# A dependent sum in VectorE's order moved behind one other instruction

## The chip, the cores and the metric

The kernel runs on one core of one Trainium2 chip. A core has a matrix engine (TensorE, PE in the profile), a vector engine (VectorE, DVE), a scalar engine (ScalarE, ACT), GpSimd (POOL) and SyncE (SP), each with its own queue of instructions that it works off in order, and sixteen DMA engines that move data between HBM and the core's memory. The metric is the device time of one execution in microseconds (us), as a median over runs.

## What is computed

Two layers of a bidirectional encoder over 256 tokens of width 4096. What matters here is the shape of the large products, all in float32:

```python
for l in range(DEPTH):                       # DEPTH = 2
    h = rmsnorm(x, norm_w[l])
    proj = h @ w_in[l]                       # (256 x 4096) @ (4096 x 11264)
    aq, ak, av, ag, rq, rk, rv, rg = jnp.split(proj, SPLIT_POINTS, axis=-1)
    a_out = silu(ag) * gqa_attention(rope(norm(aq)), rope(norm(ak)), av)
    r_out = silu(rg) * rmsnorm(bidirectional_retention(rope(rq), rope(rk), rv))
    x = x + concat(a_out, r_out) @ w_out[l]  # (256 x 4096) @ (4096 x 4096)
return rmsnorm(x, final_norm)
```

The two weight matrices are nearly all of the input, and each of their elements is read once.

## The kernel before

**Products.** The depth of 4096 is cut into 16 pairs of 128-row slices (NP = 16), the output columns into blocks of two times 512, the tokens into two halves of 128. One pair of one block is a 2 x 2 by 2 x 2 product of blocks. For some pairs it is done with eight block products, for the others ("seven" pairs) with seven, after a Winograd scheme: there the weights' four blocks, in two pages "raw" and "other", are also combined into two more pages on VectorE, called wsum in the profile: v (tag T, one subtraction over 128x1024), and u (tag U, two instructions over 128x512). With a the raw page and b the other one, u's first half is a[1] + v[0], and its second half is u's first half minus b[1]. So v, the first half and the second half are a chain, each step reading what the step before it wrote.

**Precision.** A float32 operand is split into a rounded high part and the remainder. ScalarE casts the high part (whi, or whb for a half page), VectorE subtracts to get the low part (wlo, wlb), and TensorE does three products of 512 columns per block product: whi with the operand's high part, whi with its low part, wlo with the high part. So each weight page costs one cast on ScalarE and one subtraction on VectorE. For pages called "far", ScalarE makes fhi and the negative flo, and a DMA that adds, issued by GpSimd, completes flo.

**The token operands** (x7h, x7l, x8h, x8l, xmh, xml) are made once for each of the four phases (in and out projection of two layers) by `split_pair` (L929): for a seven pair VectorE makes four sums s1 to s4 into a page xf, ScalarE casts the high parts, and VectorE subtracts the low parts.

**What sets the order.** Python code plans the whole program once, before anything runs. `run` keeps one clock for each engine (class `Clock`, with costs of instructions), always takes the engine that is free first, and `pick` (L867) records the next instruction for it. Work on weights is held in lists of `Op`s by engine, sorted by due time; `Weights.best` (L754) looks at the first LOOK = 4 entries of VectorE's list and takes the first that is ready. Everything else (combining the seven products M1 to M7 at the end of a block, rotary tables, attention, retention, operand splits) runs as `Lane`s, that are put between the weight work by their due times or their urgency. The chip then runs each engine's list in that order, with semaphores where data or a buffer is waited for. A wait on one row of VectorE holds all rows behind it.

**Buffers.** There are six raw pages of 512 KB (RAWS), four whi (HIGHS), three wlo (LOWS), one pair of half pages (HALVES), two wsum pages (SUMS) and two far pages (FAR). A raw page's next load is issued by SyncE's queue when its last reader is done. The raw page of a seven group has two readers that count: u and wlo.

In `Weights.make_u`, that is the whole step before:

```python
ve.tensor_add(u[:, 0, :], a[:, 1, :], v[:, 0, :])
ve.tensor_sub(u[:, 1, :], u[:, 0, :], b[:, 1, :])
g.u = (u, Ready(now, ve.done))
```

Of the kernel before, what the change touches and what calls it, by code (L numbers as in the profile page):

```python
# [40 lines left out]
HALVES = 1  # L41
SUMS = 2
FAR = 2
LOOK = 4
DUE_LEAD = 25.0
RUSH, SPLIT_LEAD = 2.8, 6.0
SUMS_PACE = 7.0
# [3 lines left out]
SUM_LEAD = 2.0  # L51
# [176 lines left out]
class Clock:  # L228


    def __init__(self, engine, cost, lap, now):
        self._engine, self._cost, self._lap, self._now = engine, cost, lap, now
        self.until, self._wrote = 0.0, None

    @property
    def done(self):
# [2 lines left out]
    def __getattr__(self, name):  # L239
        call = getattr(self._engine, name)  # L240

        def recorded(out, *args, **kwargs):
            self.until = max(self.until, self._now.t)
            if self._wrote and any(meet(self._wrote, extent(v)) for v in sources(args, kwargs)):
                self.until += self._lap + OWN_PASS
            self.until += self._cost(name, out, args, kwargs) - self._lap
            self._wrote = extent(out)
            return call(out, *args, **kwargs)  # L248

        return recorded  # L250
# [70 lines left out]
def extent(v):  # L321
    return v.tensor.name, v.offset, v.offset + sum(step * (n - 1) for step, n in list(v.ap)[1:])
# [24 lines left out]
def hybrid_encoder(  # L347
# [17 lines left out]
    ve = Clock(nc.vector, vector_cost, 0.083, now)  # L365
# [29 lines left out]
    def f32(v):  # L395
        return v.bitcast(F32)
# [37 lines left out]
    one = t(cp, [P, P], "one")  # L434
# [98 lines left out]
    class Weights:  # L533


        def __init__(self):
            self.pages, at = [], 0.0
            for phase in range(2 * DEPTH):
                w = w_out if phase % 2 else w_in
                for b in range(N_OUT2 if phase % 2 else N_IN):  # L540
                    start = (phase, b) == (0, 0)
                    end = (phase, b) == (2 * DEPTH - 1, N_OUT2 - 1)
                    for n, (p, k, uses) in enumerate(pages_in_order(phase, start, end)):
                        g = Page()
# [12 lines left out]
            self.lows, self.halves = Slots(LOWS), Slots(HALVES)  # L557
            self.holds = {"x7": Slots(0), "x8": Slots(0)}
            self.todo, self.ops = [], {"V": [], "A": [], "F": []}
            at = {}  # L560
            for g in self.pages:
                if g.direct:
                    self.todo.append((g.at, g, "raw", g.kind == PAGE_B))
                    continue
                if not g.seven:
                    self.todo.append((g.at - (FAR_LEAD if g.far else 0.0), g, "raw", g.kind == PAGE_B))
                    if g.far:
                        self.op("F", g, FAR_LEAD, self.far_ready, self.far_parts)
                    else:
                        self.op("A", g, HIGH_LEAD, self.high_ready, self.high)  # L570
                        self.op("V", g, 0.0, self.low_ready, self.low)
                    continue
                if g.kind == PAGE_A:
                    a = g
                    a.raw = a.other = a.v = a.u = None
                    a.reads = {PAGE_A: 2, PAGE_B: 2}
                    self.todo.append((g.at, a, "raw", 0))
                    self.todo.append((g.at + 0.01, a, "other", 1))
                    self.op("V", a, SUM_LEAD, self.v_ready, self.make_v)
                    self.op("V", a, SUM_LEAD - 0.01, self.u_ready, self.make_u)  # L580
                g.a = a
                self.op("A", g, HIGH_LEAD, self.high_ready, self.high)
                self.op("V", g, 0.0, self.low_ready, self.low)
            self.todo.sort(key=lambda v: v[0])
            for v in self.ops.values():
                v.sort(key=lambda o: o.key)
            self.at, self.adds, self.landed = 0, [], {}

        def place(self):
            return self.pages[self.at].at if self.at < len(self.pages) else 1e9  # L590
# [29 lines left out]
        def make_v(self, g):  # L620
            self.sums.take()
            a, b = f32(g.raw[0]), f32(g.other[0])
            v = t(wp, [P, 2, NB], "wsum", SUMS)
            ve.tensor_sub(v, a, b[:, 0:1, :].to_broadcast([P, 2, NB]))
            g.v = (v, Ready(now, ve.done))

        def u_ready(self, g):
            return g.v is not None and self.sums.ready()

        def make_u(self, g):  # L630
            self.sums.take()
            a, b, v = f32(g.raw[0]), f32(g.other[0]), g.v[0]
            u = t(wp, [P, 2, NB], "wsum", SUMS)
            ve.tensor_add(u[:, 0, :], a[:, 1, :], v[:, 0, :])
            ve.tensor_sub(u[:, 1, :], u[:, 0, :], b[:, 1, :])
            g.u = (u, Ready(now, ve.done))
            for k in (PAGE_A, PAGE_B):
                g.reads[k] -= 1
                if not g.reads[k]:
                    self.raws.give(ve.done)  # L640
# [113 lines left out]
        def best(self, engine):  # L754

            if engine == "A":
                ops = [o for o in self.ops["A"][:1] + self.ops["F"][:1] if o.ready()]
            else:
                ops = [o for o in self.ops["V"][:LOOK] if o.ready()][:1]
            return min(ops, key=lambda o: o.key, default=None)  # L760

        def make(self, one):
            self.ops[one.engine].remove(one)
# [2 lines left out]
    weights = Weights()  # L766
# [99 lines left out]
    def pick(e):  # L866
        if e == "P":  # L867
            if step_lane("P", lanes + running()):
                return True
            if main[1] is not None and main[1]():  # L870
                progress[0] = now.t
                main[1] = next(main[0], None)
                return True
            return False
        if step_lane(e, urgent):
            return True
        w = weights.best(e)
        splits = [v for v in waiting[:SPLITS] if v.ready(e)]
        soon = splits[0] if splits else None
        hurry = [v for v in lanes + running() if v.ready(e) and v.urge()]  # L880
        first = min((v for v in lanes + running() if v.ready(e)), key=lambda v: v.due, default=None)
        if soon and (w is None or soon.key - SPLIT_LEAD < w.key):
            soon.step()
        elif first and w and first.due < w.key:
            first.step()
        elif hurry and (w is None or w.key > weights.place() + RUSH):
            hurry[0].step()
        elif w:
            weights.make(w)
        else:  # L890
            return step_lane(e, splits + lanes + running())
        clear()
        return True
# [40 lines left out]
    def split_pair(p, v, phase, gains):  # L934

        def tokens(v):

            return v.rearrange("p k (a t) -> p k a t", t=BLK)

        x0, x1 = v[:, 0], v[:, 1]  # L940
        if gains is not None:
            yield "A"
            for i in range(2):
                u = v[:, :, i].rearrange("p m a t -> p (a m) t" if phase else "p m a t -> p m (a t)")
# [4 lines left out]
        if seven:  # L949
            yield lambda: not sums_of and held[0] + sum(max(0, v.need - v.own) for v in tasks if v.begun) < PAGES  # L950
            sums_of.append(p)
            hi, lo = (t(ap, [P, blocks, P], tag + s, n, F32R) for s in "hl")
# [4 lines left out]
            ac.copy(tokens(hi[:, 0:2, :]), x0)  # L957
            yield "V"
            ve.tensor_sub(s1, a22n, x1[:, 0])
            ve.scalar_tensor_tensor(s2, s1, -1.0, x0[:, 0], op0=ALU.mult, op1=ALU.subtract)  # L960
            ve.tensor_sub(s3, x0[:, 0], x1[:, 0])
            ve.tensor_sub(s4, x0[:, 1], s2)
            yield "A"
            ac.copy(hi[:, 2:7, :], f)
            yield "V"
            ve.tensor_sub(tokens(lo[:, 0:2, :]), x0, tokens(f32(hi)[:, 0:2, :]))
            ve.tensor_sub(lo[:, 2:7, :], f, f32(hi)[:, 2:7, :])
            sums_of.pop()
            drop()
        else:  # L970
            hi, lo = (t(ap, [P, blocks, P], tag + s, n, F32R) for s in "hl")
            u = [w[:, :4].rearrange("p (i m) (a t) -> p i m a t", i=2, t=BLK) for w in (hi, lo)]
            g = [tokens(w[:, 4:6]) for w in (hi, lo)]
# [1078 lines left out]
```

## Time and profile before

| | |
|---|---|
| median of 3 runs | 2584.46 us (2583.87 to 2585.4) |
| the profiled execution | 2583.31 us, of which the span from the first to the last instruction is 2581.3 us |
| granted TensorE clock, mean | 0.998 of full |
| TensorE busy | 2565.5 us, 99% of the span |
| VectorE busy | 2318.1 us, 90% |
| ScalarE busy | 1912.0 us, 74% |
| GpSimd busy | 445.3 us, 17% |
| DMA | 727.53 MB, 282 GB/s; its packets took 91.8% of the time of sixteen engines |

A matmul row of the timeline gives start and duration. Matmuls overlap in TensorE's pipeline: one of 512 columns is shown 0.39 us long, and the next one starts 0.23 us after it. So time that TensorE loses is best read from the distance between two starts, and only a part of it is shown as an idle time in brackets. On VectorE the shown durations overlap as well: a row that doesn't read what the row before it wrote starts about 0.08 us before that one's shown end. In the names, "wsum<-wraw" over 1024 elements is v, "wsum<-wraw,wsum" u's first half, "wsum<-wsum,wraw" its second half. L248 is the line of `Clock.recorded`, through which all VectorE and ScalarE work goes, L1170 that of the large matmuls, L372 that of most DMA issues.

### The profile page before, as it was taken

The page shows a single profiled execution, that of the slowest core. Times are in us where ns is not written, and L with a number is a line of the kernel's source. Part 1 is how long each engine was busy: PE and PEld are TensorE (multiplying, and loading weights), DVE is VectorE, ACT ScalarE, POOL GpSimd, SP SyncE. Part 2 cuts the span into 40 slices and gives each one's busy share as a digit, 9 for nine tenths or more (in the row PEclk, how much of TensorE's full clock was granted, in tenths as well). Part 3 has the DMA queues.
Part 4 walks back from the last instruction along what each step waited for, and adds up shares of the span by engine and source line. Part 5 has one row for each costly group of instructions (what it writes and reads, how often), then busy time and mean ns, then how long its engine had stood idle before and what let it go on. Part 6 is the DMA issues. An engine that isn't in the chain of part 4 may idle for free.

```text
span 2581.3 us, 34363 instructions
## 1 busy us (share of the span) xinstructions
PE 2565.5 (99%) x11474; PEld 2115.5 (82%) x11474; DVE 2318.1 (90%) x2911; ACT 1912.0 (74%) x2680; POOL 445.3 (17%) x604
## 2 busy tenths in 40 slices
PE   9999999999999999999999999999999999999998
PEld 5888888888888888888888888888888888888886
DVE  7999988998888899888998989989989888998887
ACT  8777776777777688766887776767778777876765
POOL 0022211221222110121112121212212121101111
PEclk9999999999999999999999999999999999999999
DMA  9999988998998898999999998989989998989997
GB/s 321 306 283 300 290 271 284 280 301 265 286 290 266 279 285 246 288 292 291 306 302 281 291 283 272 277 283 289 294 274 284 279 282 261 289 250 288 269 263 232
DMA packets 212739, 727.53 MB, mean 282 GB/s; under 512 B 25536, under 2 KB 32320, under 8 KB 212560
## 3 DMA queue, kind: packets, MB, share of 16 engines
q1 hardware_dynamic: 146464, 519.21, 56.9%
q0 software_dynamic: 66096, 206.11, 34.6%
q8 instruction: 90, 1.47, 0.2%
q14 instruction: 89, 0.73, 0.1%
HBM read 676.99 MB, written 48.23 MB: 281 GB/s over the span
## 4 chain that ended last, share of the span: by engine, by line
PE 92%; issue 2%; DMA 2%; DVE 2%; ACT 1%; POOL 0%; SPq 0%; POOLq 0%; DVEq 0%; ACTq 0%
PE M L1170 89%; PE ps L1170 3%; DMA wraw<-in_w_in 1%; DVE wlo L248 1%; DMA flo<-in_w_in 1%; DMA full<-in_xT 0%; DVE wsum L248 0%; ACT whi L248 0%; POOL out L1864 0%; ACT full L248 0%; PE ps L1009 0%; DVE x8l L248 0%; ACT fhi L248 0%; DVE x7l L248 0%; DVE xf L248 0%
## 5 line engine op out<-in xcount | busy, mean ns | idle before, releaser
L248 ACT CAST whi<-wraw 128x1024 fp32r<-128x1024 f32 (+1 forms) x521 | 540.7, 1046 | 196.7 <-PE M L1170 126.5
L248 DVE TENSOR_TENSOR wlo<-wraw,whi 128x1024 fp32r<-128x1024 f32 (+1 forms) x521 | 629.6, 1215 | 48.7 <-PE M L1170 24.3
L248 DVE TENSOR_TENSOR wlo<-wsum,whi 128x1024 fp32r<-128x1024 f32 x432 | 526.8, 1220 | 97.0 <-PE M L1170 94.2
L248 ACT CAST whi<-wsum 128x1024 fp32r<-128x1024 f32 x432 | 453.5, 1050 | 149.7 <-PE M L1170 107.0
L1170 PE MATMUL M<-whi,x7h 128*128 128x512 f32 x1248 | 486.6, 390 | 0.0
L1170 PE MATMUL M<-whi,x7l 128*128 128x512 f32 x1248 | 485.7, 389 | 0.0
L1170 PE MATMUL M<-whi,x8h 128*128 128x512 f32 x1048 | 408.2, 389 | 0.0
L1170 PE MATMUL M<-whi,x8l 128*128 128x512 f32 x1048 | 408.0, 389 | 0.0
L1170 PE MATMUL M<-wlo,x7h 128*128 128x512 f32 x1248 | 386.6, 390 | 1.5 <-DVE wlo L248 1.5
L1170 PE MATMUL M<-fhi,x8h 128*128 128x512 f32 x840 | 327.3, 390 | 0.0
L1170 PE MATMUL M<-fhi,x8l 128*128 128x512 f32 x840 | 327.0, 389 | 0.0
L372 POOL DMA_DIRECT2D flo<-in_w_in x157 | 139.6, 889 | 997.4 <-ACT flo L248 916.1
L1170 PE MATMUL M<-wlo,x8h 128*128 128x512 f32 x1048 | 309.0, 389 | 1.1 <-DVE wlo L248 1.0
L248 ACT CAST fhi<-wraw 128x1024 fp32r<-128x1024 f32 (+1 forms) x215 | 224.3, 1043 | 109.4 <-PE M L1170 62.8
L1170 PEld LDWEIGHTS M<-wlo,x7h 128*128 128x128 f32 x1248 | 233.2, 188 | 51.0 <-DVE wlo L248 3.4
L248 DVE TENSOR_TENSOR wsum<-wraw 128x1024 f32<-128x1024 f32 x216 | 263.3, 1219 | 12.9 <-DMA wraw<-in_w_out 5.9
L1170 PEld LDWEIGHTS M<-whi,x7l 128*128 128x128 f32 x1248 | 234.3, 188 | 49.1 <-issue 0.5
L1170 PEld LDWEIGHTS M<-whi,x7h 128*128 128x128 f32 x1248 | 234.3, 188 | 48.9 <-ACT full L248 0.2
L248 ACT ACTIVATE flo<-fhi 128x1024 fp32r<-128x1024 f32 (+1 forms) x215 | 226.6, 1054 | 8.3 <-ACT fhi L248 1.7
L1170 PEld LDWEIGHTS M<-wlo,x8h 128*128 128x128 f32 x1048 | 196.3, 188 | 42.5 <-DVE wlo L248 2.0
L1170 PEld LDWEIGHTS M<-whi,x8l 128*128 128x128 f32 x1048 | 196.8, 188 | 40.7
L1170 PEld LDWEIGHTS M<-whi,x8h 128*128 128x128 f32 x1048 | 196.8, 188 | 40.4 <-ACT whi L248 0.3
(281 smaller groups left out, 3785.8 us busy)
## 6 DMA issues: line engine op xcount, KB each, us to landing
wraw<-in_w_in SPq DMA_DIRECT2D x703, 512.0 KB, 5.9
wraw<-in_w_out SPq DMA_DIRECT2D x256, 512.0 KB, 6.3
flo<-in_w_in POOLq DMA_DIRECT2D x157, 512.0 KB, 8.5
flo<-in_w_out POOLq DMA_DIRECT2D x54, 512.0 KB, 8.6
full<-next_dram POOLq DMA_DIRECT2D x18, 512.0 KB, 10.3
p_dram<-room POOLq DMA_DIRECT2D x64, 128.0 KB, 3.5
pT<-p_dram POOLq DMA_DIRECT2D x16, 512.0 KB, 9.6
next_dram<-room POOLq DMA_DIRECT2D x40, 128.0 KB, 6.2
```

Source lines behind the costliest of these rows:

```text
L248: return call(out, *args, **kwargs)
L372: getattr(nc, name).dma_start(to, src, **kw)
L1170: nc.tensor.matmul(out, a, b, start=start, stop=stop)
```

## The change

Three edits, all in the planner or in the order of the code; no instruction is added or removed on any engine.

1. u's second half becomes an entry of its own in VectorE's list (`end_u`), right behind the first. `Weights.chained` tells whether the first ready entry would read what VectorE's latest instruction wrote, for the pairs v, u's first half and u's first half, u's second half; `Clock` counts its calls for that. If so, `best` takes the next ready entry, if there is one, and `pick` lets an urgent lane go ahead.
2. LOOK goes from 4 to 5.
3. In `split_pair`, s3 is computed between s1 and s2, and the low part of the two plain blocks (x7l over 256 elements) between s2 and s4 instead of ahead of the last low part.

```diff
-LOOK = 4
+LOOK = 5
...
             self._wrote = extent(out)
+            self.calls += 1
             return call(out, *args, **kwargs)
...
                     self.op("V", a, SUM_LEAD - 0.01, self.u_ready, self.make_u)
+                    self.op("V", a, SUM_LEAD - 0.02, lambda g: g.u_part is not None, self.end_u)
...
             g.v = (v, Ready(now, ve.done))
+            self.fresh = ve.calls, self.make_u
...
             ve.tensor_add(u[:, 0, :], a[:, 1, :], v[:, 0, :])
+            g.u_part = u
+            self.fresh = ve.calls, self.end_u
+
+        def end_u(self, g):
+            u, b = g.u_part, f32(g.other[0])
             ve.tensor_sub(u[:, 1, :], u[:, 0, :], b[:, 1, :])
...
-                ops = [o for o in self.ops["V"][:LOOK] if o.ready()][:1]
+                ops = [o for o in self.ops["V"][:LOOK] if o.ready()]
+                ops = (ops[1:] if len(ops) > 1 and self.chained(ops[0]) else ops)[:1]
             return min(ops, key=lambda o: o.key, default=None)
+
+        def chained(self, one):
+            return one is not None and self.fresh == (ve.calls, one.go.func)
...
-        elif hurry and (w is None or w.key > weights.place() + RUSH):
+        elif hurry and (w is None or w.key > weights.place() + RUSH or weights.chained(w)):
...
             ve.tensor_sub(s1, a22n, x1[:, 0])
+            ve.tensor_sub(s3, x0[:, 0], x1[:, 0])
             ve.scalar_tensor_tensor(s2, s1, -1.0, x0[:, 0], op0=ALU.mult, op1=ALU.subtract)
-            ve.tensor_sub(s3, x0[:, 0], x1[:, 0])
+            ve.tensor_sub(tokens(lo[:, 0:2, :]), x0, tokens(f32(hi)[:, 0:2, :]))
             ve.tensor_sub(s4, x0[:, 1], s2)
...
             yield "V"
-            ve.tensor_sub(tokens(lo[:, 0:2, :]), x0, tokens(f32(hi)[:, 0:2, :]))
             ve.tensor_sub(lo[:, 2:7, :], f, f32(hi)[:, 2:7, :])
```

Since the planner's clocks then run otherwise, rows move on every engine. u's second half stood right behind its first half in all 216 groups before. Now it does in 31; in 169 there is one other row between, in 16 there are two to five. In 151 of the 169 that row is a wlo of a raw page. On TensorE the rows are the same; small products of attention and retention stand some large matmuls earlier or later, the first one at row 951.

VectorE at the end of a block of layer 1 (the profile of before has it at 1120 to 1129 us): v of the next group (wsum_10363), the combining of M6, M7, M3, M5, M4 and M2 into ca and cb, u (wsum_10399) and the low part of the next block's first page, which is made from wraw_10261. Before:

```order
L248 TENSOR_TENSOR wsum_10363<-wraw_10261,wraw_10306 128x1024
L248 TENSOR_TENSOR wlo_10374<-wraw_10234,whi_10357 128x1024
L248 TENSOR_TENSOR cb_10349<-ca_10348,M6_9811 128x512
L248 TENSOR_TENSOR ca_10348<-cb_10349,M7_9773 128x512
L248 TENSOR_TENSOR cb_10349<-cb_10349,M3_9730 128x512
L248 TENSOR_TENSOR wsum_10399<-wraw_10261,wsum_10363 128x512
L248 TENSOR_TENSOR wsum_10399<-wsum_10399,wraw_10306 128x512
L248 TENSOR_TENSOR cb_10349<-ca_10348,M5_9745 128x512
L248 TENSOR_TENSOR cb_10349<-cb_10349,M5_9745 128x512
L248 TENSOR_TENSOR ca_10348<-ca_10348,M4_9750 128x512
L248 TENSOR_TENSOR wlo_10424<-wraw_10261,whi_10367 128x1024
L248 TENSOR_TENSOR ca_10348<-ca_10348,M2_9758 128x512
```

The same place of the changed kernel:

```order
L249 TENSOR_TENSOR wsum_10363<-wraw_10261,wraw_10309 128x1024
L249 TENSOR_TENSOR wlo_10374<-wraw_10235,whi_10357 128x1024
L249 TENSOR_TENSOR cb_10349<-ca_10348,M6_9809 128x512
L249 TENSOR_TENSOR ca_10348<-cb_10349,M7_9775 128x512
L249 TENSOR_TENSOR cb_10349<-cb_10349,M3_9730 128x512
L249 TENSOR_TENSOR wsum_10399<-wraw_10261,wsum_10363 128x512
L249 TENSOR_TENSOR wlo_10407<-wraw_10261,whi_10367 128x1024
L249 TENSOR_TENSOR cb_10349<-ca_10348,M5_9747 128x512
L249 TENSOR_TENSOR cb_10349<-cb_10349,M5_9747 128x512
L249 TENSOR_TENSOR ca_10348<-ca_10348,M4_9752 128x512
L249 TENSOR_TENSOR ca_10348<-ca_10348,M2_9758 128x512
L249 TENSOR_TENSOR wsum_10399<-wsum_10399,wraw_10309 128x512
```

The low part that the next block begins with stands four rows ahead of where it stood, and u's second half stands behind M2.

VectorE at another block's end (1285 to 1293 us of the profile), the last of layer 1; the names are as above. Before:

```order
L248 TENSOR_TENSOR wsum_11901<-wraw_11777,wsum_11868 128x512
L248 TENSOR_TENSOR wsum_11901<-wsum_11901,wraw_11795 128x512
L248 TENSOR_TENSOR cb_11854<-ca_11853,M5_11149 128x512
L248 TENSOR_TENSOR cb_11854<-cb_11854,M5_11149 128x512
L248 TENSOR_TENSOR ca_11853<-ca_11853,M4_11154 128x512
L248 TENSOR_TENSOR wlo_11931<-wraw_11777,whi_11870 128x1024
L248 TENSOR_TENSOR ca_11853<-ca_11853,M2_11161 128x512
```

In the changed kernel:

```order
L249 TENSOR_TENSOR wsum_11909<-wraw_11777,wsum_11876 128x512
L249 TENSOR_TENSOR cb_11857<-ca_11856,M5_11151 128x512
L249 TENSOR_TENSOR cb_11857<-cb_11857,M5_11151 128x512
L249 TENSOR_TENSOR ca_11856<-ca_11856,M4_11158 128x512
L249 TENSOR_TENSOR wsum_11909<-wsum_11909,wraw_11796 128x512
L249 TENSOR_TENSOR ca_11856<-ca_11856,M2_11161 128x512
L249 TENSOR_TENSOR wlo_11943<-wraw_11777,whi_11874 128x1024
```

Here u's second half stands three rows later, and the low part of the first page has gone behind M2.

VectorE ahead of the first block's end (78 to 88 us of the profile), where the token operands are still being made: full_143 is a page of tokens, x7l_672 and x8l_675 are low parts of its two pairs, wsum_868 is v of the next group. Before:

```order
L248 TENSOR_TENSOR wlb_781<-wraw_612,whb_771 128x512
L248 TENSOR_TENSOR wlo_788<-wsum_704,whi_750 128x1024
L248 TENSOR_TENSOR x7l_672<-full_143,x7h_671 128x256
L248 TENSOR_TENSOR x7l_672<-xf_673,x7h_671 128x640
L248 TENSOR_TENSOR wlo_809<-wraw_661,whi_792 128x1024
L248 TENSOR_TENSOR x8l_675<-full_143,x8h_674 128x256 x2
L248 TENSOR_TENSOR full_143<-full_143 128x256
L248 TENSOR_TENSOR wlo_832<-wsum_737,whi_805 128x1024
L248 TENSOR_TENSOR wlo_843<-wraw_679,whi_828 128x1024
L248 TENSOR_TENSOR x8l_675<-full_143,x8h_674 128x256
L248 TENSOR_TENSOR wsum_868<-wraw_790,wraw_824 128x1024
```

In the changed kernel:

```order
L249 TENSOR_TENSOR x8l_675<-full_143,x8h_674 128x256 x2
L249 TENSOR_TENSOR full_143<-full_143 128x256
L249 TENSOR_TENSOR wlb_788<-wraw_613,whb_776 128x512
L249 TENSOR_TENSOR wlo_795<-wsum_709,whi_752 128x1024
L249 TENSOR_TENSOR wlo_806<-wraw_667,whi_793 128x1024
L249 TENSOR_TENSOR x7l_672<-xf_673,x7h_671 128x640
L249 TENSOR_TENSOR x8l_675<-full_143,x8h_674 128x256
L249 TENSOR_TENSOR wlo_830<-wsum_736,whi_810 128x1024
L249 TENSOR_TENSOR wlo_843<-wraw_684,whi_832 128x1024
L249 TENSOR_TENSOR wsum_865<-wraw_797,wraw_820 128x1024
```

The operand rows have moved ahead of the weight rows, and the last x8l no longer stands right in front of v; on ScalarE the cast x8h_674 that it waits for stands right behind x7h_671, eight rows further ahead.

More of the change, by code (lines that the diff above doesn't have):

```diff
@@ L232, in __init__ @@
         self._engine, self._cost, self._lap, self._now = engine, cost, lap, now
-        self.until, self._wrote = 0.0, None
+        self.until, self._wrote, self.calls = 0.0, None, 0
     @property
@@ L574, in __init__ @@
                     a = g
-                    a.raw = a.other = a.v = a.u = None
+                    a.raw = a.other = a.v = a.u = a.u_part = None
                     a.reads = {PAGE_A: 2, PAGE_B: 2}
@@ L587, in __init__ @@
             self.at, self.adds, self.landed = 0, [], {}
+            self.fresh = None
         def place(self):
```

## Prediction

> **What bounds the kernel now.** I read the page's busy times first, then the chain that ended last, then who waited for whom on TensorE.
>
> ```profile
> span 2581.3 us, 34363 instructions
> PE 2565.5 (99%) x11474; PEld 2115.5 (82%) x11474; DVE 2318.1 (90%) x2911; ACT 1912.0 (74%) x2680; POOL 445.3 (17%) x604
> ...
> PE 92%; issue 2%; DMA 2%; DVE 2%; ACT 1%; POOL 0%; SPq 0%; POOLq 0%; DVEq 0%; ACTq 0%
> ```
>
> ```profile
> PE M L1170 <- DVE wlo L248: 2.5, 4, 1.0
> PE ps L1989 <- DVE whi L1986: 1.5, 1, 1.5
> ```
>
> TensorE is busy for 99% of the span and 92% of the last chain lies on it. The change leaves its instructions as they are, so the time can fall only by what TensorE now loses, and rise only by what it would newly lose. VectorE's 90% counts where TensorE waits for one of its rows, which it did in four places.
>
> What TensorE loses I read from distances between starts, since shown idle is too short. Undisturbed matmuls of this width start 0.23 us apart; these six pairs do not:
>
> ```profile
> 29.60 0.39 PE L1170 MATMUL M<-whi,x7l 128*128 128x512 f32 x1
> 30.40 0.73 PE L1170 MATMUL M<-wlo,x7h 128*128 128x512 f32 x2 [0.41 <-DVE wlo L248]
> ...
> 91.92 0.39 PE L1170 MATMUL M<-whi,x8l 128*128 128x512 f32 x1
> 93.35 0.50 PE L1170 MATMUL M<-wlo,x8h 128*128 128x512 f32 x1 [1.03 <-DVE wlo L248]
> ...
> 957.29 0.39 PE L1170 MATMUL M<-fhi,x8l 128*128 128x512 f32 x1
> 957.72 0.50 PE L1170 MATMUL M<-flo,x8h 128*128 128x512 f32 x1
> ...
> 1127.97 0.39 PE L1170 MATMUL M<-whi,x7l 128*128 128x512 f32 x1
> 1128.63 0.73 PE L1170 MATMUL M<-wlo,x7h 128*128 128x512 f32 x2 [0.27 <-DVE wlo L248]
> ...
> 1291.60 0.39 PE L1170 MATMUL M<-whi,x7h 128*128 128x512 f32 x1
> 1291.83 0.39 PE L1170 MATMUL M<-whi,x7l 128*128 128x512 f32 x1
> 1293.03 0.73 PE L1170 MATMUL M<-wlo,x7h 128*128 128x512 f32 x2 [0.81 <-DVE wlo L248]
> ...
> 1371.94 0.39 PE L1170 MATMUL M<-fhi,x8l 128*128 128x512 f32 x1
> 1372.43 0.50 PE L1170 MATMUL M<-flo,x8h 128*128 128x512 f32 x1
> ```
>
> The distances less 0.23 are 0.57, 1.20, 0.20, 0.43, 0.97 and 0.26 us; the first matmul after a wait is shown 0.11 us longer (0.50 against 0.39), which comes on top. So the six cost 0.68, 1.31, 0.31, 0.54, 1.08 and 0.37 us, 4.3 in all; smaller ones I put at 1 us, which makes some 5.3 us. That is the most this change could win inside the span, against 0.2% of 2584.46, which is 5.2 us. About 0.2% is also what a measurement of this kernel can tell from no change. The work after TensorE's last matmul has the same VectorE order as before and gives nothing.
>
> **The bubble.** What a dependent neighbour costs on VectorE shows at a block's end:
>
> ```profile
> 1124.24 0.69 DVE L248 TENSOR_TENSOR wsum<-wraw,wsum 128x512 f32<-128x512 f32 x1
> 1124.96 0.69 DVE L248 TENSOR_TENSOR wsum<-wsum,wraw 128x512 f32<-128x512 f32 x1
> 1125.57 0.68 DVE L248 TENSOR_TENSOR cb<-ca,M 128x512 f32<-128x512 f32 x1
> 1126.16 0.68 DVE L248 TENSOR_TENSOR cb<-cb,M 128x512 f32<-128x512 f32 x1
> 1126.76 0.68 DVE L248 TENSOR_TENSOR ca<-ca,M 128x512 f32<-128x512 f32 x1
> 1127.36 1.22 DVE L248 TENSOR_TENSOR wlo<-wraw,whi 128x1024 fp32r<-128x1024 f32 x1
> ...
> L248 DVE TENSOR_TENSOR wsum<-wsum,wraw 128x512 f32<-128x512 f32 x216 | 149.5, 692 | 7.5
> ```
>
> u's second half starts 0.72 us after its first, an independent row of the same size 0.60 us after the row ahead of it: 0.12 us. (The last row groups all 216 of these: busy time and mean ns, then the idle time before them.) The change parts 185 of the 216 pairs (order of the changed kernel), 22 us of VectorE's time. The operand sums add one bubble for each of some 30 splits, under 4 us. In total about 26 us come off an engine that is idle for 263 us already (2581.3 less 2318.1). By themselves they are worth nothing: TensorE hides them wherever it doesn't wait for VectorE. So I price only the places where it waits.
>
> The Trainium skill, "VectorE: DVE Perf Modes", section "The DRAIN you can't avoid", says that the next instruction does not start until the pipe is empty, whether instructions are chained or not; its section "Rules for kernel authors" advises fewer instructions, not other chains. By that rule no bubble would go. The rows above disagree (0.72 against 0.60 us).
>
> **Place by place**, all against the profiled execution (2583.31 us, 2.0 us more than its span):
>
> *Start (30.40).* The four operand sums, two x8l, their difference and this wlo follow each other before and after; now the x7l row is among them and one bubble is out, but another x7l has left the same run of rows. TensorE restarts with the end of that wlo, so smaller waits ahead of it only move into this one. I take -0.1 us, between -0.3 and +0.3 (one row of 128x256 more or less).
>
> *First block's end (93.35).*
>
> ```profile
> 79.65 0.42 DVE L248 TENSOR_TENSOR x7l<-full,x7h 128x256 fp32r<-128x256 f32 x1
> 79.98 0.82 DVE L248 TENSOR_TENSOR x7l<-xf,x7h 128x640 fp32r<-128x640 f32 x1
> 80.72 1.22 DVE L248 TENSOR_TENSOR wlo<-wraw,whi 128x1024 fp32r<-128x1024 f32 x1
> ...
> 86.69 0.42 DVE L248 TENSOR_TENSOR x8l<-full,x8h 128x256 fp32r<-128x256 f32 x1 [1.35 <-ACT x8h L248]
> 87.03 1.22 DVE L248 TENSOR_TENSOR wsum<-wraw 128x1024 f32<-128x1024 f32 x1
> ...
> 92.07 2.35 DVE L248 TENSOR_TENSOR wlo<-wraw,whi 128x1024 fp32r<-128x1024 f32 x2
> ...
> 81.97 3.73 SPq L372 DMA_DIRECT2D wraw<-in_w_in  x3
> ```
>
> The wlo at 92.07 comes 1.2 us too late, behind an unbroken run that begins with an x8l for which VectorE stood still for 1.35 us. In the new order that x8l's cast is eight ScalarE rows earlier and the x8l no longer heads the run, so the 1.35 us go. What could keep v late is its second raw page: its load is the first of those at 81.97, issued when the wlo at 80.72 released a page. The two x7l rows of 0.42 and 0.82 us are no longer right ahead of that wlo, so the load moves forward about as far. Taken: -1.0 us; bounds 0 (v doesn't move) and -1.31 (all of it).
>
> *1128.63.* The first page's wlo goes ahead of u's second half and three combining rows, from 1127.36 to about 1124.85; TensorE asks for it at 1128.20. Its cast is done, since VectorE didn't wait for it. Taken: -0.5; bounds -0.54 and 0. The price: u's second half starts behind M2, at 1124.24 + 0.61 + 1.14 + 4 x 0.60 = 1128.39 instead of 1124.96, 3.4 us later.
>
> *1293.03.*
>
> ```profile
> 1291.16 0.68 DVE L248 TENSOR_TENSOR ca<-ca,M 128x512 f32<-128x512 f32 x1
> 1291.76 1.22 DVE L248 TENSOR_TENSOR wlo<-wraw,whi 128x1024 fp32r<-128x1024 f32 x1
> 1292.89 0.68 DVE L248 TENSOR_TENSOR ca<-ca,M 128x512 f32<-128x512 f32 x1
> ```
>
> Here the change works against itself: the awaited wlo goes behind M2, 0.60 us more, one bubble less, so from 1291.76 to 1292.24. VectorE has been without idle time, so if it comes earlier M2 must still wait for TensorE's block to end. Taken: +0.4; bounds +0.2 and +0.6.
>
> *957.72 and 1372.43.* These wait for a DMA that completes flo, behind a far page that TensorE itself had to free; that chain has no VectorE row in it. Taken 0, bounds -0.3 and +0.3 each.
>
> *New waits.* Attention and retention rows move on all engines. I count one new wait of the size of the one at 957.72: +0.3, between 0 and four of them (+1.2).
>
> *u later, everywhere.* In 151 groups u's second half starts 1.02 us later (a wlo of 1.14 ahead of it, the bubble of 0.12 gone), and the casts of u behind it. The tightest group of the 216:
>
> ```profile
> 2553.15 0.69 DVE L248 TENSOR_TENSOR wsum<-wsum,wraw 128x512 f32<-128x512 f32 x1
> ...
> 2553.87 1.06 ACT L248 CAST whi<-wsum 128x1024 fp32r<-128x1024 f32 x1 [0.63 <-DVE wsum L248]
> ...
> 2557.36 0.39 PE L1170 MATMUL M<-whi,xmh 128*128 128x512 f32 x1
> ```
>
> u is done at 2553.84, its cast at 2554.93, TensorE reads it at 2557.36: 2.4 us to spare, so 1.02 costs nothing. The cover is ScalarE's lead over TensorE; u more than 2.4 us later would cost the excess here. Raw pages: with wlo ahead, their last reader ends 0.12 us sooner in those groups, so SyncE's loads come no later; at 1128 it ends at 1129.08 instead of 1128.58, 0.5 us later.
>
> Sum: -0.1 - 1.0 - 0.5 + 0.4 + 0 + 0.3 = -0.9 us, 2582.4 us for the profiled execution. That execution lies 1.15 us under the median, so the forecast for the median is 2584.46 - 0.9 = 2583.6 us. The terms' ends add up to -2.6 and +2.7 us, so its own range is 2581.9 to 2587.2.
>
> **Rivals.**
>
> *Slower: u behind the combining rows starves ScalarE's queue.* In 16 groups u has two to five rows ahead of it, up to 3.4 us more. ScalarE waits for it in order, and every cast behind it is late. For it: the tightest group has only 2.4 us; a delay of 3.4 us would cost 1.0 there. Against it: that group isn't one of the sixteen, and elsewhere the lead is longer. It decides from 2.4 us of delay on. At half a microsecond in each of the sixteen it costs 8 us: 2592.
>
> *Hidden anyway.* v's load doesn't move, so the 1.0 us at 93.35 stay, and the rest cancels out: about 2584.6.
>
> *All waits go.* The six waits and the small ones vanish, since VectorE has 26 us more room: 2584.46 - 5.3 = 2579.2. Against it: 1293.03 gets worse, and two of the six wait for a DMA.
>
> *The bubble stays*: whatever stands behind u's first half starts 0.72 us after it. Then the moves alone act, and the three places with a moved row get 0.12 us less each: 2583.6 + 0.3 = 2583.9. The 0.60 us between the other rows of the same run speak against it. This is the case in which the page named above would be right.
>
> *Waits elsewhere.* The new order is worse at handovers between blocks that were just in time, by 2 to 4 us in all: 2587.
>
> **How the numbers follow.** Forecast 0.66, hidden anyway 0.10, bubble stays 0.02 and waits elsewhere 0.06 all lie within 0.2%: 0.84 for the same. All waits gone: 0.04, faster. u starving ScalarE: 0.12, slower. The range reaches from 2580.5, short of "all waits go" but a little past the forecast's own end, to 2588.0, past the waits elsewhere and into the slower case.
>
> **What would show it.** In the changed profile: VectorE's busy time 15 to 25 us less; wsum<-wsum,wraw with about 1 us of idle before it instead of 7.5 (31 pairs left of 216); no wait near 92 and 1128; a wait near 1292 that is longer than 0.81; TensorE's busy time the same; the last matmul about 1 us earlier. I am wrong if TensorE waits for whi (never before), if SyncE's waits for wsum grow into late loads and ScalarE's into late casts, or if the waits for wlo add up to more than before.

## The result and the profile after

| | before | after |
|---|---|---|
| median (22 runs each) | 2584.72 us (2583.54 to 2588.12) | 2589.37 us (2587.63 to 2593.96) |
| ratio, 95% interval | 1 | 1.0018 [1.0012, 1.0024] |
| the profiled execution, its span | 2583.31, 2581.3 us | 2589.84, 2588.1 us |

The changed kernel is 4.65 us slower. That is 0.18%: within the 0.2% that the forecast called the same, but above its range (to 2588.0), and the interval doesn't reach 1, so the loss is small but real. Three executions of 3899 to 4348 us (one of before, two of e12 below) are slow ones and are left out of every figure here. The two profiled executions lie 6.5 us apart, since that of before is 1.4 us under its median here and that of after 0.5 us over.

The page after, its span and busy times:

```profile
span 2588.1 us, 34425 instructions
PE 2567.3 (99%) x11474; PEld 2114.7 (82%) x11474; DVE 2302.7 (89%) x2911; ACT 1913.6 (74%) x2680; POOL 446.7 (17%) x604
```

VectorE's busy time fell by 15.4 us, and the second halves lost their idle time (1.1 us, from 7.5): the bubbles went. Two other groups of the same view sit idle for longer (the time after the bar): the low parts of u and v pages, 116.5 us where it was 97.0, and v itself, 19.1 where it was 12.9.

```profile
L249 DVE TENSOR_TENSOR wsum<-wsum,wraw 128x512 f32<-128x512 f32 x216 | 148.2, 686 | 1.1
L249 DVE TENSOR_TENSOR wlo<-wsum,whi 128x1024 fp32r<-128x1024 f32 x432 | 526.6, 1220 | 116.5 <-PE M L1183 107.4 <-ACT whi L249 3.4 <-ACT ca L249 2.8
L249 DVE TENSOR_TENSOR wsum<-wraw 128x1024 f32<-128x1024 f32 x216 | 263.5, 1220 | 19.1 <-DMA wraw<-in_w_in 15.4 <-DMA wraw<-in_w_out 2.2 <-DVE wlb L249 0.7
```

What TensorE waits for (total, times, longest, in us):

```profile
PE M L1183 <- DVE wlo L249: 3.7, 5, 1.3
PE ps L2002 <- DVE whi L1999: 1.5, 1, 1.5
PE ps L1183 <- DVE aql L249: 1.2, 2, 0.9
PE M L1183 <- DMA flo<-in_w_in: 1.1, 1, 1.1
PE ps L1183 <- DVE pTl L249: 0.8, 1, 0.8
PE M L1183 <- DVE d L249: 0.2, 1, 0.2
```

Before there were two such lines, wlo with 2.5 us and the same 1.5 for whi. The new ones are attention operands (aql, pTl), a far page (flo) and 0.2 us for d. The places of the long ones, from TensorE's rows:

```profile
59.86 0.39 PE L1183 MATMUL M<-whi,x7l 128*128 128x512 f32 x1
60.77 0.50 PE L1183 MATMUL M<-wlo,x7h 128*128 128x512 f32 x1 [0.53 <-DVE wlo L249]
...
92.97 0.39 PE L1183 MATMUL M<-whi,x8l 128*128 128x512 f32 x1
94.55 0.50 PE L1183 MATMUL M<-wlo,x8h 128*128 128x512 f32 x1 [1.19 <-DVE wlo L249]
...
704.02 0.50 PE L1183 MATMUL ps<-pTh,kv 128*128 128x512 f32 x1
705.28 0.50 PE L1183 MATMUL ps<-pTl,kv 128*128 128x512 f32 x1 [0.76 <-DVE pTl L249]
...
1294.10 0.39 PE L1183 MATMUL M<-whi,x7l 128*128 128x512 f32 x1
1295.80 0.50 PE L1183 MATMUL M<-wlo,x7h 128*128 128x512 f32 x1 [1.31 <-DVE wlo L249]
...
1374.70 0.39 PE L1183 MATMUL M<-fhi,x8l 128*128 128x512 f32 x1
1376.18 0.50 PE L1183 MATMUL M<-flo,x8h 128*128 128x512 f32 x1 [1.09 <-DMA flo<-in_w_in]
...
1895.40 0.40 PE L1183 MATMUL ps<-kv,aqh 128*128 128x256 f32 x2
1896.74 0.38 PE L1183 MATMUL ps<-kv,aql 128*128 128x256 f32 x1 [0.93 <-DVE aql L249]
...
2575.56 0.39 PE L1183 MATMUL M<-x7l,x8h 128*128 128x512 f32 x1
```

The last matmul starts 6.2 us later; in before its row is

```profile
2569.37 0.39 PE L1170 MATMUL M<-x7l,x8h 128*128 128x512 f32 x1
```

Counted as in the prediction (distance less the undisturbed one, and 0.11 for the first matmul behind a wait), the places cost 0.79 at 60, 1.46 at 93 (before 1.31), 1.14 at 704, 1.58 at 1294 (1.08), 1.36 at 1375 (0.37) and about 1.2 at 1896; one at 621 costs another 0.5, and that at 30 is 0.2 longer. The waits at 957 and 1128 are gone (0.31 and 0.54). Together that is 4.6 of the 6.2 us. The rest are waits of about half a microsecond and less. The places at 60 and 621 were not traced back to one row.

**Why there.** At 93 the awaited low part is the first of the two at 93.28, in VectorE's rows (the first row is SyncE's, of the loads):

```profile
82.39 3.88 SPq L373 DMA_DIRECT2D wraw<-in_w_in  x3
...
88.22 1.23 DVE L249 TENSOR_TENSOR wsum<-wraw 128x1024 f32<-128x1024 f32 x1 [2.48 <-DMA wraw<-in_w_in]
...
93.28 2.35 DVE L249 TENSOR_TENSOR wlo<-wraw,whi 128x1024 fp32r<-128x1024 f32 x2
```

VectorE was free early, as forecast, and then stood for 2.48 us for v's raw page. That load was issued at 82.39 us, later and not earlier than in before (81.97): the low part that frees its page now stands behind the x8l rows and starts at 81.15 instead of 80.72. At 1294 u's second half and the combining of M2 now both stand ahead of the awaited low part:

```profile
1292.72 0.68 DVE L249 TENSOR_TENSOR ca<-ca,M 128x512 f32<-128x512 f32 x1
1293.32 0.69 DVE L249 TENSOR_TENSOR wsum<-wsum,wraw 128x512 f32<-128x512 f32 x1
1293.92 0.68 DVE L249 TENSOR_TENSOR ca<-ca,M 128x512 f32<-128x512 f32 x1
1294.52 2.35 DVE L249 TENSOR_TENSOR wlo<-wraw,whi 128x1024 fp32r<-128x1024 f32 x2
```

At 704 the new plan has exchanged attention steps. In before, the retention rows of this stretch end first, at 649; their write (next_dram) is out of GpSimd's order long before the load of pT is issued. These rows are of before, of GpSimd and VectorE:

```profile
649.28 2.23 POOL L372 DMA_DIRECT2D next_dram<-room  x4 [1.38 <-DVE room L248]
686.13 0.85 POOL L372 DMA_DIRECT2D pT<-p_dram  x1
...
701.45 1.22 DVE L248 TENSOR_TENSOR pTl<-pT,pTh 128x1024 fp32r<-128x1024 f32 x1
```

After, the softmax rows go first, the retention rows end 40 us later, and pT's load stands behind their write:

```profile
689.54 2.28 POOL L373 DMA_DIRECT2D next_dram<-room  x4 [2.49 <-DVE room L249]
692.37 0.55 POOL L373 DMA_DIRECT2D pT<-p_dram  x1
...
702.91 1.05 ACT L249 CAST pTh<-pT 128x1024 fp32r<-128x1024 f32 x1 [2.62 <-DMA pT<-p_dram]
704.00 1.23 DVE L249 TENSOR_TENSOR pTl<-pT,pTh 128x1024 fp32r<-128x1024 f32 x1 [2.04 <-ACT pTh L249]
```

The load is issued 6.2 us later, and its cast starts 10.5 us after the issue; ScalarE waits 2.62 us for it, VectorE 2.04 for ScalarE, TensorE 0.76 for VectorE. (Whether the queue alone held the load back or also a page that the retention rows still held was not separated.) At 1896 it is again the order of rows: between the two remainders of q, which were neighbours before, the new plan puts four combining rows and two low parts, and TensorE needs the second:

```profile
1890.73 0.69 DVE L249 TENSOR_TENSOR aql<-q,aqh 128x512 fp32r<-128x512 f32 x1 [1.58 <-ACT aqh L249]
...
1894.86 1.22 DVE L249 TENSOR_TENSOR wlo<-wsum,whi 128x1024 fp32r<-128x1024 f32 x1
1896.00 0.69 DVE L249 TENSOR_TENSOR aql<-q,aqh 128x512 fp32r<-128x512 f32 x1
```

### The profile page after: what moved, and what is told of

The parts are those of the page before. It is cut to its first block, busy times and chain, and to the rows that moved or that the text cites. A ratio compares the mean times of both kernels' runs of the same rounds, so it can differ in the third digit from the quotient of the medians.

```text
span 2588.1 us, 34425 instructions
## 1 busy us (share of the span) xinstructions
PE 2567.3 (99%) x11474; PEld 2114.7 (82%) x11474; DVE 2302.7 (89%) x2911; ACT 1913.6 (74%) x2680; POOL 446.7 (17%) x604
## 4 chain that ended last, share of the span: by engine, by line
PE 91%; issue 3%; DMA 3%; DVE 2%; ACT 1%; POOL 1%; SPq 0%; POOLq 0%; DVEq 0%; ACTq 0%
PE M L1183 87%; PE ps L1183 3%; DMA wraw<-in_w_in 1%; DVE wlo L249 1%; DVE wsum L249 1%; DMA q<-q_dram 1%; DMA pT<-p_dram 0%; DMA full<-in_xT 0%; DMA flo<-in_w_in 0%; ACT whi L249 0%; ACT full L249 0%; PE ps L1022 0%; POOL out L1877 0%; DVE ca L249 0%; DVE x8l L249 0%
## 5 line engine op out<-in xcount | busy, mean ns | idle before, releaser
L249 ACT CAST whi<-wraw 128x1024 fp32r<-128x1024 f32 (+1 forms) x521 | 539.8, 1045 | 184.0 <-PE M L1183 133.1
L249 DVE TENSOR_TENSOR wlo<-wraw,whi 128x1024 fp32r<-128x1024 f32 (+1 forms) x521 | 632.9, 1216 | 45.3 <-PE M L1183 20.5
L249 DVE TENSOR_TENSOR wlo<-wsum,whi 128x1024 fp32r<-128x1024 f32 x432 | 526.6, 1220 | 116.5 <-PE M L1183 107.4
L249 ACT CAST whi<-wsum 128x1024 fp32r<-128x1024 f32 x432 | 453.4, 1049 | 179.1 <-PE M L1183 119.5
L373 POOL DMA_DIRECT2D flo<-in_w_in x157 | 139.6, 889 | 987.4 <-ACT flo L249 851.7
L249 ACT CAST fhi<-wraw 128x1024 fp32r<-128x1024 f32 (+1 forms) x215 | 224.3, 1043 | 105.5 <-PE M L1183 75.5
L249 DVE TENSOR_TENSOR wsum<-wraw 128x1024 f32<-128x1024 f32 x216 | 263.5, 1220 | 19.1 <-DMA wraw<-in_w_in 15.4
L249 ACT ACTIVATE flo<-fhi 128x1024 fp32r<-128x1024 f32 (+1 forms) x215 | 226.5, 1054 | 8.1 <-ACT fhi L249 0.8
```

The costliest lines, as they stand in the source:

```text
L373: getattr(nc, name).dma_start(to, src, **kw)
```

## The experiments

Theory A: the loss comes from the plan, which the new rules make anew for all engines. Theory B: it comes from u's second half itself, which stands later and makes ScalarE's casts late. Each run was measured beside the kernel before on the same chip, 10 or 11 times (e6 5 times, e10 8); differences are between medians there. The ratios weigh every execution, so they don't follow the medians to the last figure.

**Parts of the change.** The first run takes the planner's decisions from before, and only writes u's second half down behind the next row of VectorE (190 of 216 groups):

```diff
 class Clock, recorded():
...
+            if self.defer:
+                self.defer, self.late = False, lambda: call(out, *args, **kwargs)
+                return
-            return call(out, *args, **kwargs)
+            made = call(out, *args, **kwargs)
+            self.flush()
+            return made
...
 make_u():
             ve.tensor_add(u[:, 0, :], a[:, 1, :], v[:, 0, :])
+            ve.defer = True
             ve.tensor_sub(u[:, 1, :], u[:, 0, :], b[:, 1, :])
...
```

> The planner of before decides everything, and only u's second half is put behind the one row that follows it on VectorE (190 of 216 groups); the rows of TensorE, ScalarE, GpSimd and SyncE stand as before. Theory A (the loss of 4.65 us comes from the new order of the other work, not from a later u): within 1.5 us of before, VectorE busy about 15 us less. Theory B (a later u makes ScalarE's casts late): 3 to 5 us slower than before, with TensorE waits that before lacks.

The second takes edit 3 alone (the operand sums, with the planner), the third edits 1 and 2 without it; their lines stand in the change's diff.

> Only the order of the operand sums is changed (the third edit), u as before. Theory A: up to 3 us either way, with waits at the start (30 to 93 us) and at a few new places, since the planner's clocks shift. Theory B: no difference beyond 0.7 us, since u stands as before.

> The first two edits without the operand sums. Theory A: 1 to 5 us slower, the places of the waits other than in the changed kernel. Theory B: 4 to 5 us slower, the waits at the same places behind u.

The fourth leaves before's code alone and nudges a figure of the planner:

```diff
-OWN_PASS = 0.035
+OWN_PASS = 0.036
```

> The kernel before, with the planner's own figure for a dependent neighbour at 0.036 instead of 0.035: no row is moved on purpose, but some 130 rows of VectorE's order come out otherwise. Theory A: 1 to 4 us slower, from new waits at places that have nothing to do with u. Theory B: within 0.7 us of before.

| | median, us | to before, us | ratio, 95% interval | VectorE busy, us |
|---|---|---|---|---|
| e1, halves parted, plan of before | 2584.69 | -0.5 | 0.9997 [0.9988, 1.0006] | 2302.1 |
| e2, operand sums | 2586.62 | +1.4 | 1.0009 [1.0001, 1.0018] | 2317.2 |
| e3, edits 1 and 2 | 2589.43 | +4.2 | 1.0016 [1.0007, 1.0025] | 2304.5 |
| e4, nudge | 2586.37 | +1.2 | 1.0006 [0.9997, 1.0014] | 2317.9 |

e1 takes all of VectorE's saving (16.0 us) and wins or loses no measurable time. e4's difference isn't clear of the noise either, since its interval reaches 1. What TensorE waits for in e1:

```profile
PE M L1185 <- DVE wlo L257: 1.6, 4, 0.5
PE ps L2004 <- DVE whi L2001: 1.5, 1, 1.5
PE M L1185 <- ACT full L257: 0.5, 1, 0.5
PE ps L1185 <- DVE pTl L257: 0.5, 1, 0.5
```

No whi of the block products is among them (the line for whi, 1.5 us, stands in before too), so the later u makes no cast late for TensorE. B falls. The second halves sit 0.9 us idle in all, and one other row between is enough to be rid of the bubble: behind the low part at 88.50 the second half starts after 1.14 us, and the row behind it after 0.60.

```profile
L255 DVE TENSOR_TENSOR wsum<-wsum,wraw 128x512 f32<-128x512 f32 x216 | 147.8, 684 | 0.9
```

```profile
88.50 1.22 DVE L257 TENSOR_TENSOR wlo<-wraw,whi 128x1024 fp32r<-128x1024 f32 x1
89.64 0.68 DVE L255 TENSOR_TENSOR wsum<-wsum,wraw 128x512 f32<-128x512 f32 x1
90.24 0.68 DVE L257 TENSOR_TENSOR cb<-ca,M 128x512 f32<-128x512 f32 x1
```

e3, where the sums' rules plan anew, has nearly the whole loss.

**Both ends.** e5 adds to e1 the operand rows in the new order, again with the plan of before; e6 is the reverse, the plan of after with the halves adjacent:

```diff
 e5, split_pair():
+            ve.defer = True
             ve.scalar_tensor_tensor(s2, s1, -1.0, x0[:, 0], op0=ALU.mult, op1=ALU.subtract)
             ve.tensor_sub(s3, x0[:, 0], x1[:, 0])
+            nc.vector.tensor_sub(tokens(lo[:, 0:2, :]), x0, tokens(f32(hi)[:, 0:2, :]))
             ve.tensor_sub(s4, x0[:, 1], s2)
...
             yield "V"
+            ve.skip = True            # counted by the planner, not written again
             ve.tensor_sub(tokens(lo[:, 0:2, :]), x0, tokens(f32(hi)[:, 0:2, :]))
 e6, make_u() and end_u():
+            nc.vector.tensor_sub(u[:, 1, :], u[:, 0, :], b[:, 1, :])
             g.u_part = u
...
+            ve.skip = True
             ve.tensor_sub(u[:, 1, :], u[:, 0, :], b[:, 1, :])
```

> Both orders on VectorE are written down as the change wants them (the second half of u behind one other row, the operand sums as s1, s3, s2, the low part of x0, s4), but the planner decides by the tallies of before, so TensorE, ScalarE, GpSimd and the loads keep their order to the instruction. Theory A (the loss comes from the new plan): 2584.7, as the swap alone, between 2583.5 and 2585.5; VectorE busy 2300 us; no wait of TensorE over 1 us that before did not have. Theory B (the orders themselves make casts and remainders late): 2587 or more, since the operand order comes on top.

> The kernel after with one thing undone: where the planner writes the first half of u down, the second follows at once, and at the place where it had stood nothing is written; TensorE, ScalarE, GpSimd and the loads keep the order of after. Theory A: the loss stays, 2589 to 2591, with the waits at 60, 621, 704, 1294, 1375, 1896 us in place, VectorE busy 16 us more (2319). Theory B: the loss goes, 2585.

e5: 2585.45 us (+0.3; 1.0002 [0.9993, 1.0011]), VectorE busy 2301.3. A wait for flo came that before lacks, of 1.0 us, at the limit that the expectation had set; the time is still that of before. e6: 2594.05 us (+8.9; 1.0037 [1.0025, 1.005]), VectorE busy 2317.0, the loss larger than A expected. Its waits:

```profile
PE ps L1188 <- DVE aql L252: 2.6, 3, 2.1
PE M L1188 <- DVE wlo L252: 2.4, 4, 1.5
...
PE ps L1188 <- DVE D L252: 1.4, 1, 1.4
```

So the two orders of rows do not lose by themselves. Parting the halves wins 4.3 us in the plan of after (+8.9 against +4.65; by the two intervals this is known to some 3.6 us), and nothing measurable in the plan of before. The plan of after loses 8.9 us and gets about half of it back.

**Is it one place, or the draw?** Many plans are nearly equal for the planner, and which of them it arrives at is called the draw here. Other figures for the planner give other plans. Two of after:

```diff
 e7:
-OWN_PASS = 0.035
+OWN_PASS = 0.036
 e8:
-DMA_DELAY, DMA_TAIL = 2.4, 1.0
+DMA_DELAY, DMA_TAIL = 2.41, 1.0
```

> The kernel after, but the planner takes the bubble for 0.036 us where it took 0.035; nothing else. The plan comes out otherwise in some 330 rows of VectorE and 380 of TensorE. Theory A with chance (a new plan draws its waits anew): another place for the waits, time anywhere from 2585 to 2590. If instead the change itself makes each plan worse: 2589 within 1 us, with the waits at 60 and 1375 us again.

> The kernel after, but the planner takes a load's delay for 2.41 us where it took 2.4; nothing else. Chance: anywhere from 2585 to 2590, with other waits than e7. The change itself: 2589 within 1 us.

e7 took 2590.16 us (+5.1), e8 2587.33 (+2.2). In both the attention steps of layer 1 are exchanged as at 704 us, in e7 those of layer 2 as well. In e2 layer 1 alone was, in e3 both, in before and e4 neither. That suggested theory C: the exchange is the loss. It was tested with figures for which the edits stay and the exchange goes (e9, e10), with one that makes it in layer 1 without the edits (e11), and with the last clause of the pick taken out (e12):

```diff
 e9, e10, on the kernel after:
-DMA_DELAY, DMA_TAIL = 2.4, 1.0
+DMA_DELAY, DMA_TAIL = 2.42, 1.0      # e10: 2.5
 e11, on the kernel before:
-PE_PASS = 0.2
+PE_PASS = 0.198
 e12, on the kernel after:
-        elif hurry and (w is None or w.key > weights.place() + RUSH or weights.chained(w)):
+        elif hurry and (w is None or w.key > weights.place() + RUSH):
```

> The kernel after with all its edits, but the planner takes a load's delay for 2.42 us where it took 2.4. With that figure the attention steps of both layers come out in the order of before (the retention rows with their write from room ahead of the next group's softmax rows), where after had the softmax rows first. Theory C (the loss lies in that exchange of attention steps, in each layer): the waits at 621, 704, 1714 and 1896 us go, 2.9 us of them, and the time is 2586.5, between 2585 and 2587.5. Theory D (any new plan of this change costs 4 to 5 us, wherever it waits): 2589 to 2590.

> As the run before with 2.5 us for the delay: a third plan, in both layers with the attention steps in the order of before. Theory C: 2585 to 2587.5, no wait of TensorE for pTh, pTl or aql over 0.5 us near 621, 704 and 1896. Theory D: 2589 to 2590.

> The kernel before, its two sums and its operand rows untouched, but the planner takes TensorE's own pass for 0.198 us where it took 0.2. The attention steps of the first layer come out in the order of after, those of the second stay. Theory C: waits near 621 and 704 or 841 us for aql and pTh, 1 to 2 us, time 2586 to 2588. Theory D: no loss without the change's own edits, 2585.

> The kernel after without its last clause in the pick: a lane that hurries no longer goes ahead because the sum at hand is chained. Attention steps in the order of after in both layers. Theory C: 2588.5 to 2590.5, as after. If the clause carried the loss: 2585 to 2586.

e9: 2586.97 us (+1.3; 1.0007 [0.9998, 1.0016]); e11: 2586.85 (+1.2; 1.0009 [1.0, 1.0018]); e12: 2589.50 (+3.8; 1.0015 [1.0006, 1.0024]). e9 and e12 fit C, and the clause carries no measurable part of the loss. e11 fits by its time alone, which is hardly clear of the noise: of the 1 to 2 us of waits for aql and pTh that were expected, only 0.2 us for aql came. e10 doesn't fit: 2592.19 us (+6.5; 1.0026 [1.0016, 1.0036]) with the steps in the order of before. What it waits for is something else:

```profile
PE M L1183 <- DMA flo<-in_w_in: 3.5, 4, 1.3
PE M L1183 <- DVE ca L249: 2.0, 2, 1.0
PE M L1183 <- DVE wlo L249: 1.5, 3, 0.6
```

So C is at most one way of losing, not the whole cause. Sorted by the exchange, the runs keep an order all the same: with the steps as in before -0.5 to +1.3 us (and e10's 6.5), with layer 1 exchanged +1.2 to +2.2 (e2, e8, e11), with both layers exchanged +3.8 to +5.05 (after, e3, e7, e12; e6 8.9). That is no test of it, since no run exchanges both layers without edit 1. The last runs ask whether the edits make plans worse, or before had a good draw: e13 to e15 are the kernel before at the planner's figures of e8 to e10. e16 is e1 on the plan of e4 (the line of e4's diff in e1's kernel).

```diff
 e13, e14, e15, on the kernel before:
-DMA_DELAY, DMA_TAIL = 2.4, 1.0
+DMA_DELAY, DMA_TAIL = 2.41, 1.0      # e14: 2.42, e15: 2.5
```

> The kernel before, the planner's figure for a load's delay 2.41 us for 2.4: the partner of e8, which has the same figure and the change. If the edits of the change make a plan worse by themselves: 2585 to 2586, below e8 by 1.5 us or more. If it is the draw alone: 2585 to 2590, above e8 as often as below.

> As e13 with 2.42 us, the partner of e9 (2586.97). The edits make it worse: 2584.5 to 2586. The draw alone: 2585 to 2590.

> As e13 with 2.5 us, the partner of e10 (2592.19). The edits make it worse: 2584.5 to 2587. If the figure 2.5 itself brings the waits for flo and for ca at 594, 960 to 968, 1376 and 2242 to 2250 us: 2589 to 2592, with these waits in place.

> The plan of e4 (the kernel before with 0.036 us for the bubble, 2586.37) to the instruction on TensorE, ScalarE, GpSimd and the loads, and the second half of u written behind the next row of VectorE, as in e1. The saved bubbles are worth 0.5 us in the plan of before and 4.7 us in the plan of after; here e4 has waits for wlo of 3.1 us in all, so between 2584.0 and 2586.0, and VectorE busy 16 us less.

| the planner's figures | without the edits | with them | difference, us |
|---|---|---|---|
| as they were | 0 | +4.65 (after) | 4.65 |
| OWN_PASS 0.036 | +1.2 (e4) | +5.05 (e7) | 3.9 |
| DMA_DELAY 2.41 | -0.4 (e13, 2585.24) | +2.2 (e8) | 2.6 |
| DMA_DELAY 2.42 | +0.2 (e14, 2585.84) | +1.3 (e9) | 1.1 |
| DMA_DELAY 2.5 | +0.25 (e15, 2585.89) | +6.5 (e10) | 6.3 |

(Each to the runs of before beside it, and known to about 2.3 us, as the intervals show; a single difference can so be chance, and the mean of five is known to about 2.3 x 1.41 / 2.24 = 1.5.) The plan with the edits is the slower one in all five, by 3.7 us in the mean. By the draw alone each would come out faster about as often as slower, and all five slower once in 32 times. In three of the five (as they were, 0.036 and 2.41) the plan with the edits exchanges attention steps and its partner doesn't. And the figure 2.5 doesn't bring the waits of e10: e15, without the edits, has one wait for flo of 1.0 us and none for ca. So both hold at these figures: the plans with the edits lose more, and where and how much (1.1 to 6.3 us) is the draw. e16 came to 2585.62 us (0.9998 [0.9989, 1.0007]), 1.2 us less against before than e4 (within the noise) and with 15.1 us less VectorE time (2302.8): a third plan in which parting the halves does no harm.

**What stays open.** Which rule of edit 1 makes the plans worse isn't shown. The clause of e12 is out; left are the skipping of the chained entry and the second half as an entry of its own. Edit 2 was not run alone, and the exchange of attention steps not in both layers without edit 1. That the plans lean on VectorE's saved time fits e6, where taking it back cost 4.3 us, but this is argued. No version was found that beats before measurably: e1, e5, e13 and e16 equal it.

## Why the prediction was wrong

- *Bubble*: right. e1 parts 190 pairs; at 0.12 us that is 22.8 us, and there VectorE's busy time fell by 16.0 and the idle time ahead of the second halves by 6.6 (7.5 to 0.9). Worth nothing measurable by itself, as e1 and e5 show. The operand sums, put at under 4 us, gave at most 1 us of busy time (0.9 in e2, 0.8 from e1 to e5). The rival *the bubble stays* disagrees with the trace. The rule that the prediction takes from the Trainium skill's page "VectorE: DVE Perf Modes" (section "The DRAIN you can't avoid") is only half of what stands there: the section adds that a next op that is not held starts earlier. The trace agrees with that half, since independent rows of 128x512 start 0.60 us apart.
- *Start (30.40)*: -0.1 forecast, +0.2 measured, in its bounds.
- *First block's end (93.35)*: -1.0 forecast, +0.15 measured, outside the bounds. VectorE did come free earlier, but v waited 2.48 us for its raw page. The prediction named that page and expected its load to move forward by about 1 us; it was issued 0.42 us later. It holds for the rival *hidden anyway*.
- *1128.63*: -0.5, measured -0.54. *1293.03*: +0.4, measured +0.5. Where the order of rows was compared at a place, the price came out.
- *957.72 and 1372.43*: the first went (-0.3), the second cost 1.0 us more, three times its bound. flo's load, issued at 1368.10, was awaited until 1376.18, 8.1 us, against 6.5 in before (issued 1365.89, awaited until 1372.43). That the load's own time would hold was assumed without a row, and why it took longer isn't shown. The reading that this chain has no VectorE row in it was wrong for before: there ScalarE stood 1.36 us for VectorE's `room`, and the casts up to flo follow without a gap. After, the cast of fhi waits for TensorE instead. The rows of before (L248, L372) and of after (L249, L373):

```profile
1362.13 0.41 ACT L248 CAST x8h<-room 128x256 fp32r<-128x256 f32 x1 [1.36 <-DVE room L248]
...
1365.89 0.86 POOL L372 DMA_DIRECT2D flo<-in_w_in  x1 [9.29 <-ACT flo L248]
...
1365.61 1.05 ACT L249 CAST fhi<-wraw 128x1024 fp32r<-128x1024 f32 x1 [1.21 <-PE M L1183]
...
1368.10 0.85 POOL L373 DMA_DIRECT2D flo<-in_w_in  x1 [8.94 <-ACT flo L249]
```

- *New waits*: this is the step that failed. "I count one new wait of the size of the one at 957.72: +0.3, between 0 and four of them (+1.2)". Measured at 60, 621, 704 and 1896 alone: 0.79 + 0.5 + 1.14 + 1.2 = 3.6 us, four waits as the upper end had it, but of up to 1.2 us instead of 0.3. The size was taken from the smallest wait of before; those at block ends (1.31, 1.08) were as near. And it was priced as noise on a fixed plan, though the change's own order showed that rows move on all engines. (The place at 60 lies among operand rows, not attention or retention rows.) Of the 5.5 us between the forecast sum (-0.9) and the places measured (+4.6), 3.3 lie in this term, 1.15 in the first block's end and 0.7 in the two places for flo.
- *u later everywhere*: no cost, right. The rival *u behind the combining rows starves ScalarE* was given 0.12; ScalarE's idle time ahead of its casts of wsum, for VectorE's wsum, did grow from 41.8 to 57.3 us, but TensorE never waits for whi in a block product, and e1 shows no loss.
- *Waits elsewhere*, 2587 at 0.06, was the case that came nearest: 2 to 4 us forecast, 4.65 measured, only that three of its places lie in attention steps rather than at handovers between blocks.
- *What would show it*: VectorE's 15 to 25 us less (15.4), the 1 us of idle time (1.1), the longer wait near 1292 and none at 1128 came true; that the wait near 92 goes, that TensorE's busy time stays (1.8 us more) and that the last matmul comes 1 us earlier (6.2 later) did not. Waits for wlo adding up to more than before (3.7 against 2.5) had been named as a sign of error.

## What to carry to other kernels

Where a planner sets the order, two edits are made at once, the rows that were meant to move and a new plan for all engines: measure them apart, by writing the rows down in the new order under the old plan, and nudge a figure of the planner in both versions before a difference of a few microseconds is put down to the edit. A saving on an engine that isn't the bound is worth what the waits at that engine are worth, here 0.5 us of 16 under the plan of before, which is within the noise of 2.3; the rest is room that a new plan can spend, though that it does so is argued and not shown. For a new plan, a wait should be priced from the largest waits of the old one, not from the smallest.

## What the hardware showed

The same load from memory doesn't take the same time: half a megabyte of flo took 6.5 us from issue to use at one place of before, and 8.1 at the same place of after; pT's load of the same size, from another source, took 10.5 us at 692. Why they differ isn't shown. The 1.5 us between the two plans are longer than the longest row of VectorE there (1.22 us).
